# First norm of a decoder block from feature tiles alone, its sums on TensorE, and seven modulation columns moved from VectorE to GpSimd and ScalarE

## The chip, the core and the metric

The kernel runs on one core of a Trainium2 chip. The core has TensorE (matmuls, called PE in the profile, with its weight loads listed as PEld), VectorE (DVE), ScalarE (ACT), GpSimd (POOL) and SyncE (SP), which here issues nearly all transfers between the chip's main memory and the core's own memory (SBUF). TensorE writes its results to PSUM, eight banks of 512 float32 columns. The metric is the time of one execution on the device in microseconds (us); lower is better.

## The reference

One decoder block over 1024 tokens of 1024 features, in float32. A conditioning vector `c` gives six modulation vectors of 1024 features. The part of it that the change touches is the first line but one:

```python
mod = silu(c) @ w_ada + b_ada
sh1, sc1, g1, sh2, sc2, g2 = split(mod, 6)
h = x * rsqrt(mean(x * x, axis=-1) + 1e-6) * norm1_g      # one factor for each token
h = h * (1 + sc1) + sh1                                   # one scale and one shift for each feature
x = x + g1 * token_mixer(h)        # retention, dilated attention, gates; starts with h @ w_in
h = rms_norm(x, norm2_g) * (1 + sc2) + sh2
x = x + g2 * (square(relu(h @ w_ff1)) @ w_ff2)
out = rms_norm(x, norm_f_g)
```

So `h` needs a sum of squares over the 1024 features of each token, and for each feature one dot product of `silu(c)` with a column of `w_ada` for the scale and one for the shift.

## The kernel before

All activations lie transposed: a tile holds 128 features on the partitions and the 1024 tokens along the free dimension. `x` is therefore eight feature tiles `xt[k]`, k = 0 to 7, and `h` is eight pairs `hh[k]`, `hl[k]`: the value rounded to TensorE's float32 format, and the rest. Each product of the block is taken from three matmuls (high by high, high by low, low by high), so each weight tile is split in the same way, the high half by ScalarE, the low one by a VectorE subtraction.

The program's order on each engine is the order in which the code calls the instructions; no planner reorders it. `startup` (L386) is the first step, `av_first` (L779) the next four, each with two feature tiles; these eight steps multiply each `hh[k]`, `hl[k]` by the first group of attention value weights (`av_k`, L746: 24 matmuls of 512 columns for each k, into all eight PSUM banks, one bank for 128 tokens). After them two more value groups and the rest of the block follow. In detail:

- SyncE loads `c`, then eight tiles of `x` by tokens (`xn`, 128 tokens by 1024 features, L396), with small constants between them, and then for each k two tiles of `w_ada` (`early_load`, L343: the scale column tile `SC1 + k` and the shift column tile `SH1 + k`, 128 features by 1024 each) and the feature tile `xt[k]` (L348), with value weights (`raw`, L85) behind k = 0, 1 and 3.
- TensorE spreads `c` over the partitions (L410), ScalarE takes its silu into `cb` (L411). TensorE makes the bias rows of the attention (`bias_rows`, L432), ScalarE copies them out (L434).
- ScalarE squares the eight token tiles and sums each row in the same instruction (L413). VectorE turns the eight columns of sums into mean plus epsilon (L364), GpSimd raises them to the power -0.5 (L365), TensorE spreads the result over the partitions (L372), into two PSUM banks, which ScalarE later copies to `rb1` (L785).
- `mod1` (L443) multiplies a `w_ada` tile by `cb` on VectorE and sums each row in the same instruction (L448): one modulation column for 128 features. `h1_mods` (L461) adds the biases, two small VectorE instructions.
- `h1_scale` (L467) multiplies `xt[k]` by its column and by the spread factor on VectorE (L471), and ScalarE adds the shift and writes `hh[k]` (L473). `h1_low` (L475) writes `hl[k]` on VectorE (L476). The low half of a weight tile is the VectorE subtraction of L774, every second step.
- In step k of `av_first`, `h1_mods`, `h1_scale` and `h1_low` work for k + 1 and `mod1` for k + 2, so VectorE runs a step ahead of TensorE.

The tiles named here share one pool of 26 slots of 128 by 1024 float32; a tile that comes later takes the slot of one that has been read for the last time.

Of the kernel before, what the change touches and what calls it, by code (L numbers as in the profile page):

```python
# [11 lines left out]
F32 = mybir.dt.float32  # L12
F32R = mybir.dt.float32r
AF = mybir.ActivationFunctionType
# [3 lines left out]
P = 128  # L18
D = 1024
S = 1024  # L20
NK = D // P
H = 4
C = 128
NC = S // C
# [110 lines left out]
def block_kernel(ctx, tc, io, stop=None, dbg=None):  # L135
    nc = tc.nc
# [26 lines left out]
    def ps_s(name, shape=(P, 512)):  # L163
        return PS["p"].tile(list(shape), F32, tag="s", bufs=PS["n"], name=name)
# [4 lines left out]
    mods = cst.tile([P, 48], F32, name="mods")  # L169
# [162 lines left out]
    def x4(name, dt=F32):  # L332
        return xpool.tile([P, 1024], dt, tag="x", bufs=26, name=name)
# [9 lines left out]
    def early_load(k):  # L343

        for i in (SC1 + k, SH1 + k):
            early[i] = x4(f"em{i}")
            nc.sync.dma_start(early[i], io["w_ada"][i])
        nc.sync.dma_start(xt[k], io["xT"][k])  # L348

    def rstd_rows(acc, name, pool, meanwhile=None):  # L350

# [24 lines left out]
    bs1 = xpool.tile([P, NK], F32, name="bs1")  # L376
    rel = xpool.tile([P, 12], F32, name="rel")
    dsh1 = xpool.tile([P, NK // 2], F32, name="dsh1")
    ss1 = xpool.tile([P, NK], F32, name="ss1")
    first = {"lows": []}  # L380

    def bias_cut(t, g):
# [3 lines left out]
    def startup(issue, prepare, limits):  # L386
        limits = iter(limits)
        first["release"] = lambda: issue(next(limits))
        crow, orow = x4("crow")[:1], x4("orow")[:1, :P]
        nc.vector.memset(rel[32:33], 1.0)  # L390
        nc.vector.memset(orow, 1.0)
        nc.sync.dma_start(crow, io["c"])

        xn = [x4(f"xn{b}") for b in range(NC)]
        for b in range(NC):
            nc.sync.dma_start(xn[b], io["x"][b])  # L396
            if b == 1:
                nc.sync.dma_start(rel[:32], io["rel_bias"])
                for g in range(3):
                    nc.sync.dma_start(bias_cut(onehot, g)[:33], io["onehot"][:, 384 * g:384 * g + 384])  # L400
            if b == 4:
                nc.sync.dma_start(ct, io["cst"])
                nc.sync.dma_start(vec, io["vec"])
        for k in range(NK):
            early_load(k)
            if k in (0, 1, 3):
                issue((k + 3) // 2)
        for j in range(2):
            pc = ps_s(f"pc{j}")
            nc.tensor.matmul(pc, orow, crow[:, j * 512:(j + 1) * 512], start=True, stop=True)  # L410
            nc.scalar.activation(cb[:, j * 512:(j + 1) * 512], pc, AF.Silu)  # L411
        for b in range(NC):
            nc.scalar.activation(xn[b], xn[b], AF.Square, accum_out=ss1[:, b:b + 1])  # L413
        for g in range(3):
            bias_rows(g)
        rs = rstd_of(ss1, "n1", xpool)
        mod1(0)
        nc.vector.tensor_scalar_add(bs1, vec[:, VC_BADA + SC1:VC_BADA + SC1 + NK], 1.0)
        h1_mods(0)
        first["rb"] = [rstd_bcast(rs, 4 * j, 4, f"n1{j}") for j in range(2)]  # L420
        prepare(1)
        for j in range(2):
            h1_scale(0, j)
        mod1(1, (SC1,))
        h1_low(0)
        first["lows"].pop(0)()
        mod1(1, (SH1,))

    def bias_rows(g):

# [12 lines left out]
    def mod1(k, parts=(SC1, SH1)):  # L443

        for i in parts:
            i += k
            t = early[i]
            nc.vector.scalar_tensor_tensor(t, t, 1.0, cb, op0=ALU.mult, op1=ALU.mult, accum_out=mods[:, i:i + 1])  # L448

    def mod_prep(i):  # L450

# [327 lines left out]
    def av_first(kk):  # L779

        def body(ahead, w):
            for k in (2 * kk, 2 * kk + 1):
                if k == 0:
                    for j, rb in enumerate(first["rb"]):
                        nc.scalar.copy(rb1[:, 512 * j:512 * j + 512], rb)  # L785
                if k % 2 == 0:
                    ahead(1)
                if k + 1 < NK:
                    h1_mods(k + 1)
                    h1_scale(k + 1)  # L790

                    if first["lows"]:
                        first["lows"].pop(0)()
                        h1_low(k + 1)
                        if k + 2 < NK:
                            mod1(k + 2)
                    elif k + 2 < NK:
                        mod1(k + 2, (SC1,))
                        h1_low(k + 1)
                        mod1(k + 2, (SH1,))  # L800
                    else:
                        h1_low(k + 1)
                av_k(0, k, w)
                if k == 3:
                    first["release"]()
                if k == 4:
                    for g in range(3):
                        bias_out(g)
                if k == NK - 1:
                    ahead(1)  # L810
                    if first["lows"]:
                        first["lows"].pop(0)()
                    nc.sync.dma_start(cs, io["cossin"])
                    nc.sync.dma_start(decay, io["decay"])
        return body
# [1587 lines left out]
def pack(x, c, w_ada, b_ada, norm1_g, w_in, rel_bias, ret_gn_g, ret_gn_b,  # L2403
         w_ret_out, w_att_out, w_o, norm2_g, w_ff1, w_ff2, norm_f_g):
    A = np.asarray
    w = A(w_in)[0]
    att = w[:, 6144:10752].reshape(1024, 3, 3, 512)
    gates = lambda js: np.concatenate([w[:, 10752 + P * j:10752 + P * j + P] for j in js], axis=1)
    a = {
        "xT": np.ascontiguousarray(A(x)[0].T).reshape(NK, P, S),  # L2410
        "c": A(c).reshape(1, D),
        "x": A(x)[0].reshape(NC, P, D),
        "w_ada": np.ascontiguousarray(A(w_ada)[0].T).reshape(48, P, D),
        "vec": np.ascontiguousarray(np.concatenate(
            [_vec(A(norm1_g)[0]), _vec(A(norm2_g)[0]), _vec(A(norm_f_g)), _vec(A(b_ada)[0]),
             _vec(A(ret_gn_g)[0]), _vec(A(ret_gn_b)[0])], axis=1)),
        "rel_bias": A(rel_bias),
        "w_rq": _pairs(w[:, 0:1024]),
        "w_rk": _pairs(w[:, 1024:2048]),
        "w_rv": _vblocks(w[:, 2048:4096]),  # L2420
        "w_rg": _cols(w[:, 4096:6144]),
        "w_aq": _pairs(att[:, :, 0].reshape(1024, 1536)),
        "w_ak": _cols(att[:, :, 1].reshape(1024, 1536)),
        "w_av": _vcols(att[:, :, 2].reshape(1024, 1536), 512),
        "w_gate": _cols(gates(i for c in COVER for i in c)),
        "w_gate2": _pairs(gates(GATES)),
        "w_ret_out": _blocks(A(w_ret_out)[0]),
        "w_att_out": _k4(A(w_att_out)[0]),
        "w_o": _cols(A(w_o)[0]),
        "w_ff1": _pairs(A(w_ff1)[0]),  # L2430
        "w_ff2": _k4(A(w_ff2)[0, 3072:]),
        "w_ff2s": _quads(A(w_ff2)[0, :3072]),
    }
    a.update(_constants())
    return a
# [17 lines left out]
```

## Time and profile before

| | us |
|---|---|
| time, median of 3 runs | 2243.01 |
| lowest, highest | 2242.38, 2244.39 |
| profiled execution, span from first to last instruction | 2248.9 |
| TensorE busy in it | 2183.6 (97%) |
| VectorE busy | 1455.3 (65%) |
| ScalarE busy | 908.6 (40%) |
| GpSimd busy | 145.6 (6%) |

The profile is of one execution apart from the timed ones; it tells of this execution its span alone, which is 5.9 us above the median of the runs. A row of a timeline gives the start in us from the first instruction, the duration in us, engine, source line and operation, the output tile and the tiles read, shapes (partitions by elements) and the number of instructions merged into the row; in brackets, the engine's idle time before it and what ended that. A row of a list by tile or by line gives the shortest, median and longest duration in ns and the first and last start in us. A float32 matmul is carried out as two, each with its own weight load, so counts of these are double those in the code. Matmuls overlap: the distance of their starts is what one costs, not the duration.

### The profile page before, as it was taken

The numbers are of one execution on the slowest core, as the hardware profiler recorded it, in microseconds if no ns is written. First come the engines' busy times: TensorE is split into PE (matmuls) and PEld (weight loads), VectorE is DVE, ScalarE is ACT, GpSimd is POOL, SyncE is SP. The second block draws the span as 40 slices with busy tenths as digits, with TensorE's granted clock in tenths as the row PEclk, the third lists the DMA queues.
The fourth block names the chain that finished last, engine by engine and source line by source line (L and its number), as shares of the span: only waits on it lengthen the run. The fifth ranks groups of instructions, "written<-read, shape, count | busy, mean of one in ns | idle before, by whom it ended". The sixth has DMA issues, their size and how long they took to land.

```text
span 2248.9 us, 27131 instructions
## 1 busy us (share of the span) xinstructions
PE 2183.6 (97%) x10130; PEld 1808.0 (80%) x10130; DVE 1455.3 (65%) x2285; ACT 908.6 (40%) x1665; POOL 145.6 (6%) x168
## 2 busy tenths in 40 slices
PE   7999999999999999999999999999999999999998
PEld 5887888887877888887788788888778888888887
DVE  6527777753548778853554554576866665787845
ACT  4323333223334445534634633434454445533412
POOL 0001111000011122100000000002100000000003
PEclk9999999999999999999999999999999999999999
DMA  9648999625775556549723345645134443745322
GB/s 361 197 145 277 289 284 287 198 93 178 246 271 169 168 181 206 191 165 241 207 78 94 105 178 210 247 156 178 61 136 155 155 155 145 266 151 169 122 85 76
DMA packets 154371, 408.93 MB, mean 182 GB/s; under 512 B 27062, under 2 KB 54973, under 8 KB 149822
## 3 DMA queue, kind: packets, MB, share of 16 engines
q1 hardware_dynamic: 148542, 363.14, 46.3%
q0 software_dynamic: 5696, 44.04, 8.2%
q8 instruction: 80, 1.31, 0.2%
q14 instruction: 53, 0.43, 0.1%
HBM read 316.27 MB, written 156.13 MB: 210 GB/s over the span
## 4 chain that ended last, share of the span: by engine, by line
PE 47%; DVE 5%; ACT 2%; DMA 2%; issue 1%; SPq 0%; POOL 0%; POOLq 0%; DVEq 0%; ACTq 0%
PE fp L201 4%; PE fp L203 4%; PE fp L205 4%; PE f2a L203 2%; PE f2a L205 2%; PE f2a L201 2%; PE ak L201 1%; PE ak L203 1%; PE ak L205 1%; PE wo L201 1%; PE wo L205 1%; PE wo L203 1%; PE roa L203 1%; PE roa L201 1%; PE roa L205 1%
## 5 line engine op out<-in xcount | busy, mean ns | idle before, releaser
L201 PE MATMUL qap<-hh,qaw 128*128 128x512 f32 x216 | 84.3, 390 | 3.9 <-ACT qat L280 2.2
L205 PE MATMUL qap<-hh,qaw 128*128 128x512 f32 x216 | 84.1, 389 | 0.0
L203 PE MATMUL qap<-hl,qaw 128*128 128x512 f32 x216 | 84.0, 389 | 0.0
L614 POOL TENSOR_TENSOR j<-qk,j 128x512 fp32r<-128x512 f32 x32 | 43.4, 1356 | 470.2 <-ACT j L613 470.2
L1912 ACT ACTIVATE a<-a 128x512 f32<-128x512 f32 x48 | 30.3, 631 | 79.1 <-DVE a L1911 79.1
L1266 ACT ACTIVATE P<-P,ng 128x128 f32<-128x128 f32 (+1 forms) x96 | 41.9, 438 | 41.8 <-DVE ng L1263 41.8
L1809 POOL TENSOR_TENSOR accnf<-accnf,sqnf 128x256 f32<-128x256 f32 (+1 forms) x18 | 16.6, 922 | 619.0 <-ACT sqnf L1808 619.0
L258 DVE TENSOR_TENSOR fw<-w1r,fw 128x512 fp32r<-128x512 f32 x48 | 33.0, 688 | 36.3 <-ACT fw L248 36.3
L2098 ACT CAST w2h<-w2s 128x512 fp32r<-128x512 f32 x36 | 22.4, 621 | 77.6 <-DVE w2s L2136 75.3
L201 PEld LDWEIGHTS qap<-hh,qaw 128*128 128x128 f32 x216 | 40.5, 188 | 13.2 <-ACT qat L280 2.6
L201 PE MATMUL fp<-h2h,fw 128*128 128x512 f32 x128 | 50.0, 390 | 0.0
L203 PE MATMUL fp<-h2l,fw 128*128 128x512 f32 x128 | 49.8, 389 | 0.0
L205 PE MATMUL fp<-h2h,fw 128*128 128x512 f32 x128 | 49.8, 389 | 0.0
L201 PE MATMUL roa<-rh,rwl 128*128 128x512 f32 x128 | 49.8, 389 | 0.0
L203 PE MATMUL roa<-rl,rwh 128*128 128x512 f32 x128 | 49.8, 389 | 0.0
L205 PE MATMUL roa<-rh,rwh 128*128 128x512 f32 x128 | 49.8, 389 | 0.0
L636 ACT COPY sm<-sT 128x128 f32<-128x128 f32 x32 | 8.5, 267 | 101.8 <-PE sT L627 100.1
L1647 DVE TENSOR_TENSOR rwl<-rwl,rwh 128x1024 fp32r<-128x1024 f32 x25 | 30.2, 1221 | 29.0 <-ACT rwh L1677 29.0
L1809 POOL TENSOR_TENSOR accn<-accn,sqn 128x512 f32<-128x512 f32 x12 | 15.5, 1296 | 491.8 <-ACT sqn L1808 491.8
L205 PEld LDWEIGHTS qap<-hh,qaw 128*128 128x128 f32 x216 | 40.5, 188 | 8.4
L203 PEld LDWEIGHTS qap<-hl,qaw 128*128 128x128 f32 x216 | 40.5, 188 | 8.3
L1204 DVE SCALAR_TENSOR_TENSOR ql<-raw,qh 128x1024 fp32r<-128x1024 f32 x12 | 14.7, 1224 | 47.6 <-ACT qh L1203 47.6
(3081 smaller groups left out, 7216.7 us busy)
## 6 DMA issues: line engine op xcount, KB each, us to landing
v<-vd SPq DMA_DIRECT2D x32, 512.0 KB, 5.4
raw<-in_w_ada_dram SPq DMA_DIRECT2D x32, 512.0 KB, 4.9
w1r<-in_w_ff_dram SPq DMA_DIRECT2D x32, 512.0 KB, 5.1
vd<-vo SPq DMA_DIRECT2D x24, 512.0 KB, 6.4
yt<-y POOLq DMA_DIRECT2D x6, 2048.0 KB, 15.0
xsd<-as SPq DMA_DIRECT2D x24, 512.0 KB, 2.7
w2r<-in_w_ff2s_dram SPq DMA_DIRECT2D x24, 512.0 KB, 7.1
em<-in_w_ada_dram SPq DMA_DIRECT2D x16, 512.0 KB, 10.2
```

The lines of the kernel that those rows point to most:

```text
L201: nc.tensor.matmul(o, wl, xh, start=first, stop=False, skip_group_check=skip)
L203: nc.tensor.matmul(o, wh, xl, start=False, stop=False, skip_group_check=skip)
L205: nc.tensor.matmul(o, wh, xh, start=False, stop=last, skip_group_check=skip)
L258: nc.vector.tensor_sub(t[:, 512:], src, fv(t[:, :512]))
L614: nc.gpsimd.tensor_sub(t[:, 1], src, fv(t[:, 0]))
L636: nc.scalar.copy(sm, ps[:, :C])
L1204: nc.vector.scalar_tensor_tensor(lo, raw, QSCALE, fv(hi), op0=ALU.mult, op1=ALU.subtract)
L1266: nc.scalar.activation(v, v, AF.Exp, bias=ng[:, blk:blk + 1], accum_out=st[:, g, blk, 2 + a:3 + a])
L1647: nc.vector.tensor_sub(lo, fv(lo), fv(hi))
L1809: (nc.vector if f == 7 else nc.gpsimd).tensor_add(G["acc", key], G["acc", key], sq)
L1912: nc.scalar.activation(o, o, AF.Relu)
L2098: nc.scalar.copy(hi, src)
```

## The change

`x` by tokens is no longer an input, and is not loaded. The feature tiles `xt[k]` are loaded where it was, ahead of `w_ada`. ScalarE squares each feature tile into a tile of its own (`sq`), and TensorE sums over the features: each squared tile is cut into eight blocks of 128 by 128, each block is the stationary operand of a matmul with one moving column of ones, and eight feature tiles accumulate in one column of PSUM for each 128 tokens, 64 calls in all. The bias rows are moved ahead of the squares. VectorE's L364 reads the sums from PSUM.

The shift columns of k = 1 to 7 are no longer made by `mod1`: GpSimd multiplies the `w_ada` tile by `cb` (`shift1`), and ScalarE sums the rows of the product with a copy (`shift1_sum`). Those of k = 0, and all scale columns, stay on VectorE.

```diff
 early_load:
         for i in (SC1 + k, SH1 + k):
             early[i] = x4(f"em{i}")
             nc.sync.dma_start(early[i], io["w_ada"][i])
-        nc.sync.dma_start(xt[k], io["xT"][k])
...
 startup:
-        xn = [x4(f"xn{b}") for b in range(NC)]
-        for b in range(NC):
-            nc.sync.dma_start(xn[b], io["x"][b])
-            if b == 1:
+        sq = [x4(f"sq{k}") for k in range(NK)]
+        for k in range(NK):
+            nc.sync.dma_start(xt[k], io["xT"][k])
+            if k == 1:
...
-            if b == 4:
+            if k == 4:
                 nc.sync.dma_start(ct, io["cst"])
                 nc.sync.dma_start(vec, io["vec"])
+        for j in range(2):
+            pc = ps_s(f"pc{j}")
+            nc.tensor.matmul(pc, orow, crow[:, j * 512:(j + 1) * 512], start=True, stop=True)
+            nc.scalar.activation(cb[:, j * 512:(j + 1) * 512], pc, AF.Silu)
+        for g in range(3):
+            bias_rows(g)
+        ss = ps_s("n1ss")
+        for k in range(NK):
+            nc.scalar.activation(sq[k], xt[k], AF.Square)
+            for b in range(NC):
+                nc.tensor.matmul(ss[:, b:b + 1], sq[k][:, b * P:(b + 1) * P], ones, start=k == b == 0,
+                                 stop=k == NK - 1, skip_group_check=True)
         for k in range(NK):
             early_load(k)
             if k in (0, 1, 3):
                 issue((k + 3) // 2)
-        for j in range(2):
-            pc = ps_s(f"pc{j}")
-            nc.tensor.matmul(pc, orow, crow[:, j * 512:(j + 1) * 512], start=True, stop=True)
-            nc.scalar.activation(cb[:, j * 512:(j + 1) * 512], pc, AF.Silu)
-        for b in range(NC):
-            nc.scalar.activation(xn[b], xn[b], AF.Square, accum_out=ss1[:, b:b + 1])
-        for g in range(3):
-            bias_rows(g)
-        rs = rstd_of(ss1, "n1", xpool)
+        rs = rstd_of(ss[:, :NC], "n1", xpool)
         mod1(0)
...
         mod1(1, (SC1,))
+        shift1(1)
         h1_low(0)
         first["lows"].pop(0)()
-        mod1(1, (SH1,))
+        shift1_sum(1)
...
+    def shift1(k):
+        t = early[SH1 + k]
+        nc.gpsimd.tensor_mul(t, t, cb)
+
+    def shift1_sum(k):
+        t = early[SH1 + k]
+        nc.scalar.activation(t, t, AF.Copy, accum_out=mods[:, SH1 + k:SH1 + k + 1])
...
 av_first:
                 if k % 2 == 0:
                     ahead(1)
+                if k + 2 < NK:
+                    shift1(k + 2)
                 if k + 1 < NK:
                     h1_mods(k + 1)
                     h1_scale(k + 1)
                     if first["lows"]:
                         first["lows"].pop(0)()
                         h1_low(k + 1)
                         if k + 2 < NK:
-                            mod1(k + 2)
+                            mod1(k + 2, (SC1,))
                     elif k + 2 < NK:
                         mod1(k + 2, (SC1,))
                         h1_low(k + 1)
-                        mod1(k + 2, (SH1,))
                     else:
                         h1_low(k + 1)
+                if k + 2 < NK:
+                    shift1_sum(k + 2)
                 av_k(0, k, w)
...
 pack:
-        "x": A(x)[0].reshape(NC, P, D),
```

1 line of the change is left out of this document (removed).

## The prediction

> **What bounds the kernel now.** I read the page first, then the busy times by stretch, then the timeline of the first stretches.
>
> ```profile
> span 2248.9 us, 27131 instructions
> PE 2183.6 (97%) x10130; PEld 1808.0 (80%) x10130; DVE 1455.3 (65%) x2285; ACT 908.6 (40%) x1665; POOL 145.6 (6%) x168
> ```
>
> TensorE is busy 97% of the span: what happens ahead of its steady work, or starves it, is paid in full, and the rest follows in the same order whenever it starts. The change touches only what comes before the second projection group. Busy times by stretch (length, then busy time and instructions of each engine, granted clock, DMA share, GB/s):
>
> ```profile
> core 0: us, PE busy (x) PEld busy (x) DVE busy (x) ACT busy (x) POOL busy (x), PEclk, DMA share, GB/s
> 0.00:16.58 16.58, 7.74 (x10) 1.85 (x10) 0.23 (x3) 11.22 (x20) 0.21 (x4) 1.00 0.89 329
> 16.58:23.12 6.54, 3.67 (x16) 3.49 (x16) 3.64 (x9) 2.97 (x5) 2.57 (x1) 1.00 1.03 410
> 23.12:31.58 8.46, 7.09 (x25) 4.76 (x25) 8.10 (x12) 3.78 (x5) 0.00 (x0) 1.00 1.03 409
> 31.58:72.66 41.08, 39.25 (x169) 31.57 (x170) 35.56 (x52) 11.41 (x13) 0.00 (x0) 1.00 0.74 263
> 72.66:115.79 43.13, 43.13 (x191) 35.69 (x191) 21.60 (x30) 18.74 (x30) 0.00 (x0) 1.00 0.67 233
> ```
>
> The borders are: the input of the reciprocal root, TensorE's first projection matmul, its second step, the end of the eight steps, and 191 matmuls behind them. In the last stretch TensorE never idles: 43.13 / 191 = 0.226 us a matmul, so 5.42 us for the 24 of a step. In the fourth, VectorE has 35.56 us of 41.08 busy, while TensorE lacks about 2. From 23.12 to 72.66 are 49.5 us for 192 matmuls that need 43.4: 6.2 us is all that a faster feeding of these steps can save. Ahead of it lie 23.12 us, in this order:
>
> ```profile
> 7.00 4.00 PE L432 MATMUL pb<-onehot,rel 33*12 33x384 f32 x6 [0.89 <-DMA onehot<-in_onehot_dram]
> ...
> 16.58 0.84 ACT L434 COPY rows<-pb 12x384 f32<-12x384 f32 x2
> 16.58 0.17 DVE L364 TENSOR_SCALAR n1rs<-ss 128x8 f32<-128x8 f32 x1 [15.48 <-ACT xn L413]
> 16.83 2.57 POOL L365 TENSOR_TENSOR n1rs<-n1rs,ct 128x8 f32<-128x8 f32 x1 [16.38 <-DVE n1rs L364]
> ...
> 17.32 0.46 ACT L434 COPY onehot<-pb 12x384 f32<-12x384 f32 x1
> ...
> 19.45 2.08 PE L372 MATMUL n10rb<-ct,n1rs 128*128 128x128 f32 x8 [8.45 <-POOL n1rs L365]
> ...
> 23.12 1.22 PE L761 MATMUL av<-raw_293h,hh 128*128 128x512 f32 x2
> ```
>
> ScalarE's squares end at 16.58; VectorE scales their sums (L364), GpSimd takes the power in 2.57 us, TensorE broadcasts it (L372), the first step follows. From L364 to the first projection matmul are 23.12 - 16.58 = 6.5 us. The steps then hang on VectorE:
>
> ```profile
> 29.06 1.28 DVE L471 SCALAR_TENSOR_TENSOR xt<-xt,a,rb 128x1024 f32<-128x1024 f32 x1
> 30.26 1.22 DVE L774 TENSOR_TENSOR raw_300l<-raw,raw_300h 128x1024 fp32r<-128x1024 f32 x1
> 31.56 1.28 DVE L476 SCALAR_TENSOR_TENSOR hl<-xt,mods,hh 128x1024 fp32r<-128x1024 f32 x1
> 32.76 1.22 DVE L448 SCALAR_TENSOR_TENSOR em<-em,cb 128x1024 f32<-128x1024 f32 x1
> ...
> 33.91 1.22 DVE L448 SCALAR_TENSOR_TENSOR em<-em,cb 128x1024 f32<-128x1024 f32 x1
> ...
> 35.50 1.28 DVE L471 SCALAR_TENSOR_TENSOR xt<-xt,a,rb 128x1024 f32<-128x1024 f32 x1
> ...
> 40.79 1.28 DVE L471 SCALAR_TENSOR_TENSOR xt<-xt,a,rb 128x1024 f32<-128x1024 f32 x1
> ```
>
> ```profile
> ACT hh L473 <- DVE xt L471: 28.7, 9, 5.3
> ```
>
> A pair of steps takes VectorE 40.79 - 29.06 = 11.73 us, TensorE 10.84. Starts lie 1.20 (L471), 1.22 (L774, as busy), 1.20 (L476) and 1.15 (L448) apart; the small ones before 35.50 take 0.45. The wait row says who feeds: ScalarE's write of the normalized tile waits 28.7 us for L471.
>
> **The change part by part.** *x by tokens is not loaded.* Eight loads go and the feature tiles take their places, so the squares find data as early as now; on SP's queue the modulation columns and projection weights behind them move up, by a load each time a feature tile drops out between them. DMA's share is about 1.0 between 16.58 and 31.58, so some 10 us of transfer go; but with the norm later (below), all that a step needs has landed before it. Price 0; if a load were late it would cost that lateness once. One load has a new dependence: the pool's storage is reused, and the last shift column's transfer has to wait until the last squared tile has been read.
>
> ```profile
> em<-in_w_ada_dram SPq DMA_DIRECT2D x16, 512.0 KB, 10.2
> ```
>
> It is wanted by the seventh multiply, 14 us after that point; 10.2 us, the landing time in the full queue, fits.
>
> *The squares.* ScalarE does eight, as before, now without reading an accumulator. They stand behind the three copies of the bias rows, and so behind TensorE's L432 matmuls, which end at 7.00 + 4.00 = 11.0; a copy takes 0.46 (17.32 row).
>
> ```profile
> L413 ACT ACTIVATE xn<-xn x8: 1043/1052/1057, 6.6 to 15.4; 128x1024 f32<-128x1024 f32 x8
> L413 ACT ACTIVATION_READ_ACCUMULATOR xn<-xn x8: 186/188/192, 7.6 to 16.4; 128x1 f32 x8
> ```
>
> The first squared tile is ready at 11.0 + 0.46 + 1.05 = 12.5.
>
> *The sums on TensorE.* 64 calls, each with its own 128 x 128 stationary tile and one moving column. The second norm does four such calls:
>
> ```profile
> L356 PEld LDWEIGHTS n21ss<-ct,accn x8: 186/192/192, 1597.9 to 1598.7; 128*128 128x128 f32 x8
> L356 PE MATMUL n21ss<-ct,accn x8: 250/250/271, 1597.9 to 1598.7; 128*128 128x1 f32 x8
> ```
>
> Four calls are 8 loads, 0.8 us from first to last: 0.114 us each at full speed. 64 calls are 128 loads: 14.6 us. That is already longer than ScalarE's eight squares (8.4), so TensorE sets the end. But these rows are deep in the kernel; at its start the array runs slower:
>
> ```profile
> L372 PEld LDWEIGHTS n10rb<-ct,n1rs x8: 288/333/338, 19.4 to 20.9; 128*128 128x128 f32 x8
> ```
>
> ```profile
> L372 PEld LDWEIGHTS n21rb<-ct,n21rs x8: 185/190/190, 1601.2 to 1602.0; 128*128 128x128 f32 x8
> ```
>
> The same broadcast has loads of 333 ns at 19.4 us and of 190 ns later. The first eight start 1.5 us apart, 0.21 each. The granted-clock column says 1.00 at both places, so I go by durations. Whether the sums speed themselves up is the question. Before them stand only the bias matmuls:
>
> ```profile
> 7.60 0.14 PEld L432 LDWEIGHTS pb<-onehot,rel 33*12 33x12 f32 x1 [0.50 <-DMA onehot<-in_onehot_dram]
> ...
> 9.52 0.14 PEld L432 LDWEIGHTS pb<-onehot,rel 33*12 33x12 f32 x1 [0.50 <-issue]
> ```
>
> From 7.60 to 9.52 they stay 0.64 us apart: four microseconds of back-to-back matmuls raised nothing. The sums stream a single column per load, less still. I take the slow price to the end: 128 x 0.21 = 27 to 27.5 us, so L364 starts at 12.5 + 27.4 + 0.3 (the last matmul, 250 ns) = 40.2 instead of 16.58: 23.6 later. The other bound is 12.5 + 14.6 + 0.3 = 27.4, 10.8 later.
>
> The Trainium skill, "TensorE: Matmul & The Clock Gate", section on the HAM clock gate, says that the array's clock is released after some 3.4 us of sustained activity. By it the sums would run slow for 3.4 to 7 us and then full, ending near 30; the bias rows above do not show it, nor does the page say how much a one-column matmul counts.
>
> While TensorE waits there, VectorE (in order, at L364) and GpSimd (at the power) stand still, with the first modulation columns, the broadcast and every GpSimd multiply queued behind. The 6.5 us to the first projection matmul stay, as the first two modulation columns still lie beside the power: it starts at 46.8.
>
> *Seven shift columns leave VectorE.* Two per pair, 1.15 each: 11.73 - 2.3 = 9.4 us, below TensorE's 10.84. Alone, this would make TensorE the bound of the steps.
>
> *Seven multiplies on GpSimd, 128 x 1024.* No such size is in the trace; the nearest:
>
> ```profile
> L1809 POOL TENSOR_TENSOR accnf<-accnf,sqnf x18: 725/742/1299, 2197.0 to 2237.7; 128x256 f32<-128x256 f32 x12, 128x512 f32<-128x512 f32 x6
> L1809 POOL TENSOR_TENSOR accn<-accn,sqn x12: 1292/1294/1302, 1520.2 to 1594.8; 128x512 f32<-128x512 f32 x12
> ```
>
> 742 ns at 256 columns and 1294 at 512 give 552 for each further 256: 2.40 us at 1024, 16.8 for seven. They wait for loads and ScalarE's conditioning only, not for the steps, so they run one behind the other from the end of the power, 40.2 + 0.25 + 2.57 = 43.0. What they do to VectorE:
>
> ```profile
> 646.33 1.47 POOL L614 TENSOR_TENSOR j<-qk,j 128x512 fp32r<-128x512 f32 x1 [219.91 <-ACT j L613]
> 648.10 1.29 POOL L614 TENSOR_TENSOR j<-qk,j 128x512 fp32r<-128x512 f32 x1 [0.30 <-ACT j L613]
> ```
>
> ```profile
> 645.43 1.22 DVE L1018 TENSOR_TENSOR vwl<-vwl,vwh 128x1024 fp32r<-128x1024 f32 x1
> 648.15 2.32 DVE L1018 TENSOR_TENSOR vwl<-vwl,vwh 128x1024 fp32r<-128x1024 f32 x1
> ```
>
> ```profile
> L1018 DVE TENSOR_TENSOR vwl<-vwl,vwh x12: 1215/1219/2318, 526.5 to 648.2; 128x1024 fp32r<-128x1024 f32 x12
> ```
>
> ```profile
> L1851 DVE SCALAR_TENSOR_TENSOR h2l<-x,mods,h2h x8: 740/743/1536, 1569.9 to 1592.5; 128x512 fp32r<-128x512 f32 x8
> ```
>
> The VectorE subtraction at 648.15 reads two SBUF tiles and takes 2.32 us against a median of 1.22; it starts with a GpSimd subtraction (1.29) and ends 1.08 after it. So it stood still until GpSimd was done. At 646.33 it is GpSimd that is longer (1.47), held by the VectorE one from 645.43. L1851, which has the form of L476, shows 1536 against 743. L448, L471 in the later steps, L774 and L476 all read two SBUF tiles. Hence GpSimd's 2.40 us stand in place of 1.15 saved.
>
> If GpSimd runs its seven through, VectorE resumes at 43.0 + 16.8 = 59.8 (the first scaling, out of PSUM, gets by) and still needs a scale column, L476, L774, the small ones and L471: 1.15 + 1.20 + 1.22 + 0.45 + 1.20 = 5.2; the write on ScalarE adds 1.15: step two starts at 66.2. The other seven steps are then TensorE's, 7 x 5.42 = 37.9: end at 104.1 against 72.66, 31.4 later. If GpSimd hid completely, step two would start 8.46 - 1.15 after the first, at 54.1, and the end be 92.0: 19.4 later. Taking turns lies between. I take 30, near the upper bound, as both rows show full standstill.
>
> *Seven sums on ScalarE.* 1.05 plus the accumulator read of 0.19 (second L413 row): 8.7 us in a stretch where it is busy 11.4 of 41. Price 0; uncovered it would be 1.24 in each step. It waits for GpSimd with the copies of the broadcast and the next write behind it; GpSimd is ahead in both readings.
>
> *Later.* From 72.66 on TensorE sets the pace without a pause (last stretch above), so nothing gives the 30 us back: span 2248.9 + 30 = 2279; the median of the runs, 2243.01, lies 5.9 below that span and moves by the same 30: 2273.
>
> **The rivals.** *The array speeds up under the sums.* For it: they are back to back over many microseconds, and the broadcast and projection matmuls from 19.45 on do get fast. Against: the bias rows. If a quarter of the loads go at 0.21 and the rest at 0.114, they take 17.7 us and L364 starts at 30.5, 10 earlier than forecast: 2263.
>
> *GpSimd blocks nothing.* For it: no row shows L448's own form beside GpSimd. Against: the 2.32 row and L1851. With the slow sums 19.4: 2262; with fast sums too, 9 later: 2252.
>
> *Not slower.* The sums hide behind the squares. This decides if a load costs under half of 0.114, so that a tile's 16 loads fit into ScalarE's 1.05 (below 0.065). The squares end at 11.5 + 8.4 = 19.9, L364 starts 3.3 later than now; with unblocked steps of 5.42 the 6.2 us come back, less the first step's slower part: 2241, within 0.2%. Against it: both prices of a load.
>
> **How the numbers follow.** Slow sums and blocking 0.54; fast sums and blocking 0.23; slow sums without blocking 0.12; both mild 0.06; not slower 0.05. Predicted is the first, 2273; its own range is 2269 to 2280 (turns taken, 20 to 31; a load at 0.23 adds 2.5; TensorE idling under the multiplies may add a slow stretch). The whole range, 2254 to 2280, takes in the next two and leaves 2252 and below out. A change under 0.2%, 4.5 us, can't be told from none: faster 0.02, same 0.03, slower 0.95.
>
> **What would show it.** In the changed kernel: 128 loads for the sums, near 0.21 us apart (0.114: first rival), the scaling of the sums starting at about 40 us; seven GpSimd multiplies of about 2.4 us with VectorE instructions of 3.5 beside them; a TensorE pause of some 10 us behind the first step; the eight steps ending near 104; from there on equal distances. Wrong I would be most if the sums ran well under 0.114 a load, or if some later idle time of TensorE took the delay up.

## The result and the profile after

The changed kernel takes 2268.89 us (median of four runs, 2267.39 to 2271.65); beside it the kernel before took 2242.70 (2241.69 to 2244.39). The ratio is 1.0117, with a 95% interval of 1.0101 to 1.0133: it is 26.2 us slower. The forecast was 2273.0 within 2254 to 2280.

The first two lines of the page of the changed kernel's profile:

```profile
span 2266.0 us, 27382 instructions
PE 2211.4 (98%) x10258; PEld 1837.0 (81%) x10258; DVE 1457.2 (64%) x2271; ACT 914.3 (40%) x1671; POOL 164.8 (7%) x175
```

The executed span is 17.1 us above the 2248.9 of the profile before, not 26. The difference lies in the execution before: a wait of TensorE in it, with the half-clock stretch behind it, is missing from a second profile of the same kernel (the first experiment below), whose span is 2240.0, and makes most of the 8.9 us between them. The row stands in the waits of TensorE between 1050 and 1090 us in the profile shown before the change:

```profile
PE gate L201 <- DVE raw_8402l L192: 6.6, 1, 6.6
```

Against the second profile the loss is 2266.0 - 2240.0 = 26.0 us, as in the medians. From here on, "before" in a comparison of traces is that second profile.

Busy times by stretch of the changed kernel, with borders that answer to those used before (L363's start, the first projection matmul, its second step, the end of the eight steps, 191 matmuls behind them):

```profile
core 0: us, PE busy (x) PEld busy (x) DVE busy (x) ACT busy (x) POOL busy (x), PEclk, DMA share, GB/s
0.00:39.67 39.67, 35.21 (x138) 29.23 (x138) 0.23 (x2) 12.50 (x15) 0.20 (x4) 1.00 0.92 351
39.67:46.29 6.62, 3.74 (x17) 3.49 (x17) 3.56 (x9) 0.72 (x1) 6.37 (x3) 1.00 0.26 79
46.29:64.06 17.77, 9.03 (x26) 6.01 (x25) 17.50 (x10) 4.87 (x8) 15.46 (x6) 0.84 0.08 30
64.06:104.45 40.39, 40.39 (x169) 33.24 (x170) 28.33 (x40) 17.31 (x24) 0.00 (x0) 0.94 0.36 102
104.45:147.74 43.29, 43.29 (x193) 35.85 (x191) 21.60 (x30) 18.88 (x30) 0.00 (x0) 1.00 0.59 212
```

The first stretch has grown from 16.58 to 39.67 us. The second is as long as before (6.62). The third, one step of the projection, has gone from 8.46 to 17.77 us, with VectorE busy for 17.50 of it and GpSimd for 15.46: the two are busy together, and much of that time is one waiting for the other, as the timeline below shows. In the fourth TensorE never pauses, but at a granted clock of 0.94. In the last it runs as it did before (43.3 us against 43.1).

The timeline of that start, changed kernel:

```profile
12.17 27.47 PE L412 MATMUL n1ss<-ct,sq 128*128 128x1 f32 x128 [1.51 <-ACT sq L410]
39.67 0.17 DVE L363 TENSOR_SCALAR n1rs<-n1ss 128x8 f32<-128x8 f32 x1 [38.58 <-PE n1ss L412]
39.92 2.57 POOL L364 TENSOR_TENSOR n1rs<-n1rs,ct 128x8 f32<-128x8 f32 x1 [39.47 <-DVE n1rs L363]
...
42.45 19.29 POOL L455 TENSOR_TENSOR em<-em,cb 128x1024 f32<-128x1024 f32 x7
42.55 2.08 PE L371 MATMUL n10rb<-ct,n1rs 128*128 128x128 f32 x8 [2.91 <-POOL n1rs L364]
...
46.29 2.55 PE L772 MATMUL av<-raw_379h,hh 128*128 128x512 f32 x6
...
47.04 1.22 DVE L451 SCALAR_TENSOR_TENSOR em<-em,cb 128x1024 f32<-128x1024 f32 x1
...
48.18 3.40 DVE L487 SCALAR_TENSOR_TENSOR hl<-xt,mods,hh 128x1024 fp32r<-128x1024 f32 x1
51.50 3.39 DVE L785 TENSOR_TENSOR raw_379l<-raw,raw_379h 128x1024 fp32r<-128x1024 f32 x1
54.81 2.35 DVE L474 TENSOR_TENSOR mods<-mods,vec 128x1 f32<-128x1 f32 x1
57.09 2.38 DVE L475 SCALAR_TENSOR_TENSOR a<-mods,bs,vec 128x1 f32<-128x1 f32 x1
59.57 3.26 DVE L482 SCALAR_TENSOR_TENSOR xt<-xt,a,rb 128x1024 f32<-128x1024 f32 x1
62.75 1.21 DVE L785 TENSOR_TENSOR raw_385l<-raw,raw_385h 128x1024 fp32r<-128x1024 f32 x1
...
64.06 0.79 PE L772 MATMUL av<-raw_379l,hh 128*128 128x512 f32 x1 [6.92 <-ACT hh L484]
```

128 matmuls take 27.47 us. Behind them come the scaling of the sums at 39.67, the power, and the seven multiplies, 19.29 us in one unbroken row. The first VectorE instruction beside them that reads two SBUF tiles, at 47.04, still takes its usual 1.22; the third multiply, which starts 0.03 later, takes 3.4 instead of 2.35. From 48.18 on it is VectorE that waits: such instructions last 3.3 to 3.4 us, and even those on a single column (L474, L475) 2.35 to 2.38 instead of 0.16 to 0.22. At 62.75, with GpSimd done at 61.74, VectorE is back at 1.21. TensorE waits 6.92 us for the second step.

The delay against before, read at the start of the same TensorE matmul in both traces, in us:

| first matmul of | before | after | later by |
|---|---|---|---|
| step one | 23.62 | 46.29 | 22.7 |
| step two | 32.07 | 64.06 | 32.0 |
| the next value group | 72.99 | 104.45 | 31.5 |
| the first retention scores (`sT`) | 663.42 | 693.37 | 30.0 |
| `rg`, right behind | 669.54 | 695.88 | 26.3 |
| end of the span | 2240.0 | 2266.0 | 26.0 |

So 31.5 us were lost by the end of the eight steps, and 5.5 of them came back some 400 to 600 us later, in code that the change does not touch.

### The profile page after: what moved, and what is told of

It reads as the page before. It is cut to its first block, busy times and chain, and to the rows that moved or that the text cites. A ratio compares the mean times of both kernels' runs of the same rounds, so it can differ in the third digit from the quotient of the medians.

```text
span 2266.0 us, 27382 instructions
## 1 busy us (share of the span) xinstructions
PE 2211.4 (98%) x10258; PEld 1837.0 (81%) x10258; DVE 1457.2 (64%) x2271; ACT 914.3 (40%) x1671; POOL 164.8 (7%) x175
## 4 chain that ended last, share of the span: by engine, by line
PE 86%; DVE 6%; DMA 3%; ACT 2%; issue 2%; SPq 0%; POOL 0%; POOLq 0%; DVEq 0%; ACTq 0%
PE av L772 5%; PE qap L203 5%; PE qap L201 5%; PE qap L205 5%; PE fp L201 4%; PE fp L203 4%; PE fp L205 4%; PE rg L201 3%; PE rg L203 3%; PE rg L205 3%; PE f2a L203 2%; PE f2a L205 2%; PE f2a L201 2%; PE ak L201 2%; PE ak L203 2%
## 5 line engine op out<-in xcount | busy, mean ns | idle before, releaser
L625 POOL TENSOR_TENSOR j<-qk,j 128x512 fp32r<-128x512 f32 x32 | 43.3, 1354 | 466.4 <-ACT j L624 466.4
L201 PEld LDWEIGHTS qap<-hh,qaw 128*128 128x128 f32 x216 | 41.0, 190 | 11.7 <-ACT qat L280 2.6
L258 DVE TENSOR_TENSOR qaw<-wa,qaw 128x512 fp32r<-128x512 f32 x54 | 36.9, 686 | 7.9 <-ACT qaw L248 7.6
```

The lines of the kernel that those rows point to most:

```text
L201: nc.tensor.matmul(o, wl, xh, start=first, stop=False, skip_group_check=skip)
L258: nc.vector.tensor_sub(t[:, 512:], src, fv(t[:, :512]))
L625: nc.gpsimd.tensor_sub(t[:, 1], src, fv(t[:, 0]))
```

## The experiments

**The kernel before once more.** No edit.

> The kernel before, unchanged, for a second profile of it. The eight projection steps ended 32.0 us later in the changed kernel's profile (first matmul of the next group at 104.45 us against 72.50), but the median moved by 26 us and the two spans only by 17. If 7 to 9 us of that difference are a stretch that only the first profile of before holds (TensorE waited 6.6 us for a low half of a gate weight near 1070 us there), this span is near 2241 us, 25 us below the changed kernel's 2266.0. If the delay of the start is really taken up by later pauses, this span is again near 2249 us.

Measured: 2241.76 us, span 2240.0. The 6.6 us wait for the low half of a gate weight is not there, and all earlier milestones agree within 1.3 us with the first profile. That one was a long execution; its excess begins at 1064 us and touches no term of the sum.

**The norm alone.** The changed kernel with all shift columns back on VectorE:

```diff
-        shift1(1)
...
-        shift1_sum(1)
+        mod1(1, (SH1,))
...
-                if k + 2 < NK:
-                    shift1(k + 2)
...
-                            mod1(k + 2, (SC1,))
+                            mod1(k + 2)
...
+                        mod1(k + 2, (SH1,))
...
-                if k + 2 < NK:
-                    shift1_sum(k + 2)
```

> Norm from feature tiles with the sums on TensorE, as in the changed kernel; all shift columns back on VectorE. Theory: the sums cost 23 us and the GpSimd multiplies some 9 more. Then the scaling of the sums starts at 39.7 us as in the changed kernel, the eight steps take their 49.5 us from the first projection matmul at 46.3, the next group starts near 95.7 us (23 later than before instead of 32), and the median lies 7 to 9 us below the changed kernel's 2269: 2260 to 2262. Rival: VectorE was the bound and the multiplies did relieve it; then this kernel is slower than the changed one by up to 6 us: 2275.

Measured: 2260.43 us (2260.06 to 2260.92), ratio 1.0087 (1.0072 to 1.0102) against 2241.40. The next value group starts at 96.59, 23.6 later than before, and step two at 55.67, 23.6 later too: the delay of the sums passes through the eight steps unchanged. The VectorE rows beside step one have their usual length:

```profile
49.16 1.28 DVE L486 SCALAR_TENSOR_TENSOR hl<-xt,mods,hh 128x1024 fp32r<-128x1024 f32 x1
54.35 1.22 DVE L784 TENSOR_TENSOR raw_385l<-raw,raw_385h 128x1024 fp32r<-128x1024 f32 x1
```

**The shift columns alone.** The kernel before, with `shift1` and `shift1_sum` as in the change, and the norm as it was.

> The start of the kernel before (x by tokens loaded, squares and sums on ScalarE); the seven shift columns multiplied by GpSimd and summed by ScalarE. Theory of the shared read: every multiply holds VectorE for about 2.4 us in place of the 1.15 saved, 8.7 us in seven, some of it given back because TensorE then sets the pace of the late steps: the next group starts 4 to 9 us later than before's 72.5, median 2247 to 2252. Rival: the multiplies lie beside VectorE's work, TensorE sets the pace at 5.42 us a step; the next group starts near 69 and the median is 3 us below before: 2240.

Measured: 2249.79 us (2248.31 to 2251.19), ratio 1.0039 (1.0024 to 1.0054). Here the multiplies come one at a time, as their tiles land, and each holds up what VectorE does beside it:

```profile
28.05 3.00 POOL L453 TENSOR_TENSOR em<-em,cb 128x1024 f32<-128x1024 f32 x1 [2.68 <-DMA em<-in_w_ada_dram]
28.71 2.35 DVE L472 TENSOR_TENSOR mods<-mods,vec 128x1 f32<-128x1 f32 x1
...
31.89 2.92 POOL L453 TENSOR_TENSOR em<-em,cb 128x1024 f32<-128x1024 f32 x1 [0.84 <-DMA em<-in_w_ada_dram]
32.49 3.40 DVE L783 TENSOR_TENSOR raw_300l<-raw,raw_300h 128x1024 fp32r<-128x1024 f32 x1
```

The next value group starts 7.5 us later than before. So the move by itself, which takes seven instructions from VectorE, makes the kernel 8.4 us slower. The two parts add: 23.6 + 7.5 = 31.1 against 31.5 at the next group, 19.0 + 8.4 = 27.4 against 26.2 in the medians.

**A busy array ahead of the sums.** The changed kernel with five long matmuls, whose result is not used:

```diff
+        warm = ps_s("warm")
+        for _ in range(5):
+            nc.tensor.matmul(warm, xt[0][:, :P], xt[0][:, :512], start=True, stop=True)
         ss = ps_s("n1ss")
```

> The changed kernel with five float32 matmuls of 128 x 128 x 512 (ten passes, results unused) between the bias rows and the sums, so that the array has streamed columns without a pause for some 7 us before the sums start near 18 us. Three theories. The sums' weight loads are slow because the array's clock is still low, and loads alone keep it up: all 128 loads lie 0.114 us apart, L363's successor starts near 33 us instead of 39.7, median about 2262. Loads with one moving column do not count as activity: loads lie 0.114 us apart for the first 3 to 10 us and then 0.21 again, the scaling starts at 38 to 43, median 2267 to 2272. The loads are slow for another reason, such as the incoming transfers: 0.21 from the first one on, the scaling starts near 46, median 2275.

Measured: 2268.01 us (2266.51 to 2269.01), ratio 1.0121 (1.0104 to 1.0138), so no gain, and the trace says why. Busy times in three stretches (the five matmuls, the first 50 loads of the sums, the rest of them):

```profile
core 0: us, PE busy (x) PEld busy (x) DVE busy (x) ACT busy (x) POOL busy (x), PEclk, DMA share, GB/s
11.00:16.00 5.00, 5.00 (x7) 2.19 (x7) 0.00 (x0) 4.74 (x6) 0.00 (x0) 1.00 1.03 409
18.00:23.90 5.90, 5.90 (x52) 5.58 (x50) 0.00 (x0) 2.24 (x3) 0.00 (x0) 1.00 1.03 410
24.00:40.80 16.80, 16.80 (x80) 16.75 (x79) 0.00 (x0) 0.00 (x0) 0.00 (x0) 0.50 0.84 326
```

The first 50 loads take 5.6 us, 0.112 each: this is the fast price, 0.114, of the second norm. The DMA share is 1.03 meanwhile, so it is not the incoming transfers that make a load slow, which was the third theory. From 23.96 us the granted clock is 0.5, for 23.9 us, and the other loads are 0.213 apart, although TensorE is busy throughout the third stretch. The last load starts at 40.4, 1.2 us later than in the changed kernel (39.2), while the first one started 5.9 later: what the fast loads gain pays for the wait for the long matmuls. Back-to-back loads with one moving column each thus do not keep the clock up that long matmuls had raised, let alone raise it: in the changed kernel they stay 0.214 apart to the end. The long matmuls needed their time too: their loads are 0.85 us apart up to 16.44 us and 0.43 from 17.22, some 6 us after the first, although the clock column shows 1.00 over this stretch as well; before its first fall it can't be taken as a measure of the pace. The Trainium skill, "TensorE: Matmul & The Clock Gate", section on the HAM clock gate, has the clock released after some 3.4 us of sustained activity, and gated again after a window of about that length without it. The trace agrees that long matmuls raise the pace, but here it took some 6 us of them; and the fall comes, 5.5 us after the first fast load, while the profile's busy column shows the array busy throughout, so what counts as activity is not what that column counts.

**GpSimd writes but does not read.** The changed kernel, with its multiplies replaced by fills:

```diff
     def shift1(k):
         t = early[SH1 + k]
-        nc.gpsimd.tensor_mul(t, t, cb)
+        nc.gpsimd.memset(t, 0.0)
```

> The changed kernel, with each of GpSimd's seven multiplies replaced by a GpSimd fill of the same 128x1024 tile with zero: GpSimd writes as much and reads nothing. This leaves out the product with the SiLU row for the shift columns 1 to 7, whose sums are then zero. Theory (VectorE is held up by what GpSimd reads from SBUF): VectorE's instructions stay at their usual 1.2 us or little more while GpSimd fills, step two starts near 54 us as in the run with the norm alone (55.7), not at 64, the next group near 92 to 96 instead of 104.5, and the time is 2256 to 2261 us. Rival (any long GpSimd instruction on SBUF holds VectorE up): instructions of 2.3 to 3.4 us beside the fills, step two near 64, time 2267 to 2270 us.

Measured: 2256.41 us (2255.46 to 2260.06), ratio 1.0067 (1.0052 to 1.0081) against 2242.24: some 12 us of the changed kernel's 26 are gone. Step two starts at 54.67, the next group at 92.75.

```profile
43.28 6.31 POOL L455 MEMSET em<- 128x1024 f32 x7
...
47.76 1.22 DVE L451 SCALAR_TENSOR_TENSOR em<-em,cb 128x1024 f32<-128x1024 f32 x1
...
48.90 1.28 DVE L487 SCALAR_TENSOR_TENSOR hl<-xt,mods,hh 128x1024 fp32r<-128x1024 f32 x1
```

The two VectorE instructions that read two SBUF tiles beside the fills take 1.22 and 1.28 us. One caution: a fill takes 0.90 us, so seven of them are over at 49.59, and only these two instructions meet them; the run takes away GpSimd's reading and two thirds of its time together. The instructions that did meet them were not held up, which the rival needed, and the seven fills last 0.95 to 0.96 us each, so that none of them waited for VectorE either. The Trainium skill, "SBUF — State Buffer", section "Who interferes with whom", states that a VectorE instruction with two SBUF inputs contends with a GpSimd instruction that reads SBUF, not with one that only writes it, and calls the port pair that they share an exclusive lock. This run, and the rows of 3.4 and 2.35 us, agree with both.

**Where the 5.5 us came back.** The traces give two places. The first is a stretch of half clock, 3.4 us long, that the kernel before has at 510 us, behind a wait of 2.1 us that both kernels have. The same 3.3 us of the program (busy times by stretch, columns as in the first such fence; before, then changed):

```profile
510.50:513.80 3.30, 3.30 (x10) 2.52 (x9) 0.17 (x1) 0.65 (x1) 0.00 (x0) 0.50 0.98 308
```

```profile
542.00:545.30 3.30, 3.30 (x16) 2.74 (x15) 0.22 (x1) 0.55 (x1) 0.00 (x0) 1.00 0.96 309
```

10 matmuls against 16: at 0.226 us each, 1.4 us. The shift-only run has this stretch too, and the norm-only run has not; but the runs below have it or not without a rule that I could find, so its cause stays open and it may be chance of the execution. (The changed kernel has such a stretch at 205 us, which the kernel before has not; a pause of 1.7 us that only the kernel before has there makes up for it.) The second place is the pause of TensorE between the first retention scores and `rg`. Before, then changed:

```profile
663.42 0.28 PE L625 MATMUL sT<-j 128*128 128x256 f32 x1
...
667.35 0.27 ACT L636 COPY sm<-sT 128x128 f32<-128x128 f32 x1 [2.38 <-DMA vd<-vr]
667.64 0.29 DVE L637 TENSOR_TENSOR sm<-sm,sT 128x128 f32<-128x128 f32 x1 [1.96 <-ACT sm L636]
...
669.00 0.48 DVE L647 SCALAR_TENSOR_TENSOR kl<-kT,ct,kh 128x256 fp32r<-128x256 f32 x1
669.54 1.22 PE L201 MATMUL rg<-hh,raw_4661l 128*128 128x512 f32 x2 [5.31 <-DVE kl L647]
```

```profile
693.37 0.28 PE L636 MATMUL sT<-j 128*128 128x256 f32 x1
...
694.81 0.26 ACT L647 COPY sm<-sT 128x128 f32<-128x128 f32 x1
695.55 0.28 DVE L648 TENSOR_TENSOR sm<-sm,sT 128x128 f32<-128x128 f32 x1
...
695.88 0.73 PE L201 MATMUL rg<-hh,raw_4724l 128*128 128x512 f32 x2 [1.71 <-DVE sm L648]
```

In the kernel before, ScalarE's copy to `sm` waits 2.38 us for a transfer out of `vr`, the earlier tile whose storage `sm` has taken; and `rg` starts behind `kl`. In the changed kernel `sm` waits for nothing, and `rg` starts behind the addition to `sm` (its end is at 695.83), not behind `kl`, which ends at 697.38 there. The following runs take this apart.

*Other storage for `sm`.* The kernel before, with the three small tiles in another pool:

```diff
-        sm = p.tile([P, C], F32, tag="sm", bufs=1, name=f"sm{h}{c}")
-        smh = p.tile([P, C], F32R, tag="smh", bufs=2, name=f"smh{h}{c}")
-        sml = p.tile([P, C], F32R, tag="sml", bufs=2, name=f"sml{h}{c}")
+        sm = right0.tile([P, C], F32, tag="sm", bufs=1, name=f"sm{h}{c}")
+        smh = right0.tile([P, C], F32R, tag="smh", bufs=2, name=f"smh{h}{c}")
+        sml = right0.tile([P, C], F32R, tag="sml", bufs=2, name=f"sml{h}{c}")
```

> The kernel before, with the three small tiles sm, smh and sml of the retention allocated in the long-lived pool instead of the retention pool, so that their storage is not that of a tile that is still being written out. Theory (5.5 us of the changed kernel's loss come back late because sm lies in other storage there): ScalarE's first copy of sm does not wait 2.4 us for the transfer of vr, TensorE pauses 1.7 us instead of 5.3 near 665 us, the slow stretch of the clock behind the pause is 3.4 us instead of 6.8, and the time is 3 to 4 us below before: 2237.5 to 2238.5. Rival (the wait moves to the next instruction on the same storage, kh on ScalarE, or the give-back had another cause): within 1 us of before.

Measured: 2240.57 us (2238.32 to 2241.42), ratio 0.9987 (0.9976 to 0.9997). The wait of `sm` is gone, but the pause only falls from 5.3 to 3.8 us, since `rg` still starts behind `kl`, and `kh`, which `kl` needs, now meets the transfer (0.44 us). So both readings were half right.

*One large tile further on.* The kernel before, so that none of these tiles lies on that storage:

```diff
         R["sl"] = R["p"].tile([P, 2, DV], F32R, name="statel")
+        R["fill"] = R["p"].tile([P, 1024], F32, name="fill")
```

> The kernel before with one unused tile of 128x1024 float32 allocated in the retention pool after its state, so that sm, smh, sml, kh and kl all lie one large tile further on, on storage whose last transfer is another one. Theory (the copy of sm, and with sm moved away the copy kh on the same storage, wait for the late transfer of vr, and this is the part of the give-back near 670 us): no wait for a transfer of vr on ScalarE there, TensorE pauses 1.7 us instead of 5.3 at the first matmul of rg, and the time is 3 to 4 us below before, 2238 to 2239. Rival (the pause comes back through another wait, or is not on the path): pause of 4 us or more, or a time within 1 us of before.

Measured: 2239.54 us (2235.95 to 2242.22), ratio 0.9988 (0.9979 to 0.9996). No wait for `vr`, and yet a pause of 3.3 us, so 2.0 of the 3.6 us come from the storage. The expected 1.7 was wrong.

*A busy array before the first broadcast.* The kernel before, with long matmuls and an early power:

```diff
+        early_pow = xpool.tile([P, 8], F32, name="earlypow")
+        nc.gpsimd.tensor_tensor(early_pow, ones.to_broadcast([P, 8]), mhalf, op=ALU.pow)
+        warm = ps_s("warm")
+        for b in (3, 4, 5, 6):
+            nc.tensor.matmul(warm, xn[b][:, :P], xn[b][:, :512], start=True, stop=True)
         rs = rstd_of(ss1, "n1", xpool)
```

> The kernel before, with two things added at its start: four 128x128x512 float32 matmuls on squared tokens (results unused) ahead of the broadcast, and one GpSimd power on constants ahead of the one that is needed. If TensorE's pace at the start is that of an array that was idle, and the first power pays for something that a second does not pay, the 16 weight loads of the broadcast take 0.11 us instead of 0.22, the power about 1.0 us instead of 2.57, and the first projection starts 2 to 4 us earlier; from there the time is 2 to 4 us less only if VectorE and the loads of the weights let step two come earlier too. If these set step two (it stood at 32.1 us with VectorE busy for 8.07 of the 8.40 us before it), the time stays within 1 us of before.

Measured: 2238.54 us (2237.98 to 2241.32), ratio 0.9985 (0.9977 to 0.9994). The two powers, and the loads of the broadcast:

```profile
11.18 1.64 POOL L418 TENSOR_TENSOR earlypow<-ct 128x8 f32<-128x8 f32 x1 [10.73 <-DMA ct<-in_cst_dram]
16.55 2.57 POOL L366 TENSOR_TENSOR n1rs<-n1rs,ct 128x8 f32<-128x8 f32 x1 [3.73 <-DVE n1rs L365]
19.18 0.97 PEld L373 LDWEIGHTS n10rb<-ct,n1rs 128*128 128x128 f32 x8 [3.63 <-POOL n1rs L366]
20.07 0.97 PEld L373 LDWEIGHTS n11rb<-ct,n1rs 128*128 128x128 f32 x8
```

Eight loads of the broadcast take 0.97 us instead of 1.78, and the first projection starts 1.7 us earlier, step two 2.5, but the next group only 1.0 (72.01; the other runs with an unchanged start have it between 72.2 and 73.0). VectorE as what holds the steps there is the likely reason, not one that a run shows. The rest of the gain comes later: the stretch of half clock at 510 us is absent, and the pause below is shorter. The second power still costs 2.57 us, so that part of the expectation was wrong. The run also did something that was not meant. TensorE's wait at the first `rg`, in the kernel before, in this run, in the one with the large tile, in the changed kernel, and in the one with both (below):

```profile
PE rg L201 <- DVE kl L647: 5.3, 1, 5.3
```

```profile
PE rg L202 <- DVE sm L643: 4.3, 1, 4.3
```

```profile
PE rg L201 <- DVE kl L648: 3.3, 1, 3.3
```

```profile
PE rg L201 <- DVE sm L648: 1.7, 1, 1.7
```

```profile
PE rg L202 <- DVE sm L644: 1.7, 1, 1.7
```

Where one PSUM tile more is in use at the start (here `warm`, in the changed kernel `n1ss`), `rg` is released by `sm`, else by `kl`. Two runs were to show this alone, with one unused PSUM tile more in the kernel with the large tile, and seven unused ones more in the changed kernel:

```diff
+        ps_s("turn")
         rs = rstd_of(ss1, "n1", xpool)
```

```diff
+        for j in range(7):
+            ps_s(f"turn{j}")
         rs = rstd_of(ss[:, :NC], "n1", xpool)
```

> The kernel before with the unused tile in the retention pool (as in the run of the same name) and one more unused PSUM tile allocated at the start, nothing else. Theory (the changed kernel allocates one PSUM tile more than before, for the sums; the eight banks are used in turn, so that everything behind it takes the next bank, and the accumulator rg then waits for the reader of sT, the addition to sm, instead of that of kT, kl): TensorE's pause at the first rg is 1.7 us, released by sm, where without the PSUM tile it was 3.3, released by kl. Rival (it was the early matmuls that moved the pause): 3.3, released by kl.

> The changed kernel with seven more unused PSUM tiles allocated at the start, so that with the one for the sums it is eight and the banks stand as before. By the same theory TensorE's pause at the first rg grows from 1.7 us, released by sm, to 3.3, released by kl, with no wait of sm for a transfer; by the rival it stays 1.7.

Measured: 2239.13 and 2271.07 us; the pauses are 3.3 us released by `kl` and 1.7 released by `sm`, as without the edit. Neither run tells the readings apart: a tile that nothing writes changed nothing, so no run here changes the bank alone.

What the traces do show is who releases the first `rg`, over all runs: `kl` in each of the six whose start uses no PSUM tile more (the two profiles of before, the shift columns alone, the two with other storage alone, and the one with the unused PSUM tile); `sm` in each of the seven with one PSUM tile more in use (among them the norm alone and the fills); and in the run with five early matmuls, where two more are in use, TensorE does not wait at the first `rg` at all. That fits the reading that `rg` takes over a bank which `kT` had in the first case (`kl` reads it last), `sT` in the second (the addition to `sm` reads it last) and neither in the third. The traces carry no bank numbers, so the bank is argued, not shown. In size, the storage is worth 2.0 us (5.3 to 3.3, shown by the run with the large tile; in the first profile of before the wait of `sm` is 1.7 us and the pause 4.6), and what comes with one PSUM tile more in use 1.6 (3.3 to 1.7; with the old storage 5.3 to 4.3, where `sm` waited 0.5 us longer for its transfer, 2.9): together the 3.6 us.

**The two gains together.** The early matmuls with `sm`, `smh` and `sml` apart, and with the large tile:

> The kernel before with the additions of the two runs before this one together (warm start, and sm, smh and sml apart): the sum of their two gains, so 2235 to 2238 us if both hold, and as the second alone (2237.5 to 2238.5) if the start is set by VectorE.

> The kernel before with the unused tile of the run before this one and the four early matmuls and the early power: 5 to 7 us below before, 2235 to 2237, if the two gains add; 2238 to 2239 if they do not.

Measured: 2236.34 us (2234.20 to 2240.30), ratio 0.9977 (0.9968 to 0.9987), and 2237.56 (2233.88 to 2245.69), ratio 0.9981 (0.9970 to 0.9992); the pause is 1.7 us in both. The gain at the start does not show in their profiles: the granted clock falls to 0.5 for 3.4 us at 20.3 us in the first and at 19.1 in the second, the first eight loads of the broadcast take 1.49 and 1.78 us instead of the 0.97 above, and the first projection starts at 23.3 and 23.2, as without the early matmuls. So the same additions do not keep the array fast in every execution, and that the two gains add rests on the medians alone. In the profiled execution of the second (span 2243.2) TensorE waited once more for the gate weight near 1065 us (3.5 us), as in the first profile of before. The first has the lowest median of this study, 5.9 us below before and 32.5 below the changed kernel. It keeps the norm and the shift columns as they were before the change.

## Why the prediction was right, and where it was not

*The sums on TensorE: right.* 27.4 us were forecast for 128 loads at 0.21, from 12.5; they ran from 12.17 for 27.47 us, and L363 (the old L364) started at 39.67 against 40.2. That the array would not speed up by itself held, but the bias rows were thin evidence for it: they last 4 us, and even long matmuls needed some 6 in the run with a busy array, so rows of 4 us could not have told. That single columns stream even less was the better argument. The first rival needed loads at 0.114 for three quarters of the sums; there was none, and even an array already at speed fell back within 5.5 us.

*From the scaling to the first projection: right.* 6.5 us forecast, 6.62 measured.

*The multiplies: right in their price, wrong in their course.* A multiply was put at 2.40 us; undisturbed in the shift-only run the first took 2.37, but beside VectorE seven take 19.29, 2.76 each. The forecast let GpSimd run its seven through, 16.8 us, with VectorE standing until 59.8. In fact they took turns: VectorE got an instruction in after each multiply from the second on, and each 3.4 us of it are a wait of some 2.2 and its own 1.2. The small instructions on one column, priced at 0.45 us in all, took 2.35 each. Step two came at 64.06 us, 2.1 earlier than the 66.2 forecast (0.5 of it from the sums).

*The other seven steps: short by 2.5 us.* 37.9 forecast, 40.39 measured. TensorE's 6.9 us wait brought 6.8 us of half clock from 61.91 on, so step two took 7.75 us (64.06 to 71.81) and the six others 5.44 each. The forecast had named such a stretch as a risk only. The two misses cancel: the eight steps end at 104.45 against 104.1. That this sum fits to 0.4 us is luck.

*The price of the hold-up.* The next group starts at 96.59 with the norm alone, 92.75 with the fills, 104.45 with the multiplies. Taking the shift columns off VectorE is thus worth 3.8 us where nothing is held up, and the hold-up costs 11.7. The second rival (GpSimd blocks nothing) put the end of the steps at 92.0, which is what the fills give and the multiplies don't.

*The step that failed: "nothing gives the 30 us back".* It was argued from a stretch in which TensorE runs without a pause, and the delay did pass through that stretch unchanged. But later pauses are not all of TensorE's own making: 3.6 us came back at the first `rg`, 2.0 of them because `sm` lies on other storage there and 1.6 where one PSUM tile more is in use at the start (by its bank, as argued above), and some 1.5 with a stretch of half clock that did not come, whose cause stays open. "I take 30" was low by 1.5, and the give-back was 5.5: 26.0 in the spans, 26.2 in the medians.

*The loads not made: price 0, as forecast.* DMA's share is 0.26 and 0.08 in the stretches from 39.67 to 64.06, and from there to the end of the eight steps no engine waits for a transfer, so everything had landed before it was needed. ScalarE's seven sums took 7 x (1.04 + 0.19) = 8.6 us beside other work, also as forecast.

*Median and span.* The move of the median by the same amount as the span was right for the amount; that the span shown was a long execution, mostly by the one wait of 6.6 us, could have been suspected from its 5.9 us above the median.

## What to carry to other kernels

Moving a sum to TensorE is cheap only if its matmuls have columns to stream: a weight load for each single column costs 0.21 us here, and keeps the clock down for as long as it lasts. Moving a product of two SBUF tiles from VectorE to GpSimd relieves VectorE only of work that it would not have to do beside it: here each GpSimd multiply cost VectorE more (up to 2.2 us in each instruction) than the 1.15 us it saved. When a change adds or drops tiles, compare what later tiles inherit, storage above all and PSUM banks with it, before putting a gain or a loss far from the change down to the change itself; a pause there can often be had, or removed, by one tile's place.

## What the hardware showed that was not expected

- One-column matmuls with full weight loads, back to back, let a raised clock fall: 0.112 us a load for 5.6 us, then a granted clock of 0.5 for 23.9 us and 0.213 a load, with TensorE busy all the time.
- VectorE instructions of 128 x 1 with two SBUF inputs wait out a GpSimd multiply like large ones: 2.35 us instead of 0.16.
- GpSimd's power of 128 x 8 costs 2.57 us also when one ran just before it (that one took 1.64, out of constants).
